# Spread row factors by a shuffle, mask the inverse in halves, rotate during the value projection, group the compression chunks by four

## Chip, cores and metric

The kernel runs on one core of one Trainium2 chip. The metric is the device time of one execution in microseconds (us), as the median of several runs. In the names of the profile, PE is the matrix engine, PEld its weight loads, DVE the vector engine, ACT the scalar engine, POOL the GpSimd engine, and SP the engine whose queue issues most DMAs.

## What is computed

One decoder block on 256 tokens of width 1024, all in float32:

```python
h = x @ w_in                      # q,k,v,z,beta,decay of DeltaNet; q, three K/V pairs, gates of NSA; merge gates
q, k = l2norm(silu(conv4(dq))), l2norm(silu(conv4(dk)));  v = silu(conv4(dv))
y_dn = gated_delta_rule(q, k, v, g, beta) ...              # chunks of 64 tokens, 8 heads
y_nsa = nsa_attention(nq, kc, vc, ksl, vsl, kwn, vwn, gates)
x = layer_norm(alpha*x + (sig(mg_dn)*(y_dn @ w_dn) + sig(mg_nsa)*(y_nsa @ w_nsa)) @ w_out)
x = layer_norm(alpha*x + (silu(u_gate) * u_val) @ w_down)  # u = conv3(x @ w_up) + b
```

Three pieces matter here. In the delta rule every chunk of 64 tokens and every head has a matrix of decays, `decay[i,j] = exp(g_i - g_j)` on a triangle, and a unit lower triangular system that is solved (`triangular_solve`). In NSA the keys and values of the compressed branch pass through `silu(blk @ w1) @ w2`, where `w1` has 4096 rows and 256 columns, once for keys and once for values. And the first 32 dims of the queries and of two sets of keys are rotated (`partial_rope`).

## The kernel before, in words

**Projections.** The order of the work is written out by hand: the list `PLAN` names 128x1024 weight chunks of 512 KB in the order in which PE uses them, and `HEAD` is its first part: `k`, `q`, `kc`, `vc`, then 16 bodies (`nq` 0 to 7, `ksl` 0 and 1, `kwn` 0 and 1, `vt` 0 to 3), each of them followed by one compression chunk `cmp`. After `HEAD` come `v`, `z`, the merge gates and the rest. Each weight chunk is loaded by SP into one of six `raw` buffers (`dma_chunk`, L167), split by ACT and DVE into a high part and a low part (`split_chunk`, L187 and L192; three buffers each), and used by 24 matmuls (`mm_feat`, L313 to L315), whose result lies in one of two PSUM buffers `pg` until ACT or DVE has read it. A new split may begin when PE is done with a chunk; a new load into `raw` when a split is done.

**Compression.** `cmp_chunk` (L775) multiplies one 128x1024 chunk of `w1`: four matmuls with 32 stationary columns each, into four groups of 32 partitions of one PSUM tile `ph`, so that the four run beside one another; each counts as two records in the profile. Eight chunks make the keys' hidden layer, eight the values'. The chunks lie in four slots in the tile `AT` (`cmp_slot`); `feed` issues their loads on SP behind the loads into `raw`.

**Fibers.** Everything else is written as generators that `pump` advances by one turn after each projection: `delta` (decays, similarities, inverse), `rope`, `cmp_end`, `attention`. `wait(name)` gives up as many turns as the tables `W` and `WAITS` say. All engines run their instructions in the order in which they were emitted; a waiting instruction holds all behind it on its engine.

**Row factors.** `delta` transposes 32 row factors per token (`rrow`, L494), writes them to DRAM (`rscr`, L498) and reads them back onto all partitions (L502, two DMAs of 512 KB into `L` and `QKT`, quarters 0 and 3 of the tile `LT`). Five turns later a mask and a column factor are added, to `L` by DVE and to `QKT` by POOL (L509, L511), ACT takes both exponentials, and the similarities are multiplied in (L521 to L528) for four groups of heads and tokens, one PSUM buffer each of the four named `ps`.

**Inverse.** POOL inverts the 16x16 diagonal blocks (L570, L572), writes the result and its transpose to DRAM (`tscr`, L577), reads them back in another layout (L580), and four turns later DVE, POOL and ACT spread them under a mask over `T` and `TT` (L588, L590).

**Rotation.** `rope` starts after `HEAD`. It loads 768 KB of cosines and sines, gathers 32 rows of `NQ` and `KC` with eight DMAs into `AT`, runs four DVE instructions of 768 columns (L734 to L739) and scatters the result with eight DMAs (L741, L743).

Of the kernel before, what the change touches and what calls it, by code (L numbers as in the profile page):

```python
# [6 lines left out]
F32 = mybir.dt.float32  # L7
# [26 lines left out]
def _slots(table, *items):  # L34
    o = 0
    for name, n in items:
# [8 lines left out]
              ("fcb", 44), ("g1", 8), ("b1", 8), ("w2", 512))  # L45
N_PA = 169
TAIL = 7
# [15 lines left out]
def plan():  # L63
# [4 lines left out]
    for j in range(NFF):  # L68
        seq += [("ug", j), ("uv", j)]
        if 0 < j <= NFF - TAIL:  # L70
# [10 lines left out]
         wc=0, sv=0, wv=0, lc=0, s3=1, s4=1, ss=0, z=0, on=0, oc=1, sim=1, vb=1, rest=0, zz=1)  # L81
WAITS = dict(back0=4, ca0=2, ca1=0, cb0=2, cb1=5, expL0=0, expQ0=0, la0=2, la2=1, la3=3, later0=0, later1=1,
             later3=2, lb0=1, lb1=2, lb2=2, lb3=0, lc0=0, lc1=0, lev0=3, mask0=5, oc0=2, oc1=1, oc2=0, oc3=0,
             on0=0, p400=2, pgm0=3, rb0=4, rest0=2, rows0=1, s10=0, s30=1, s32=1, s34=0, s36=8, s37=0, s41=2,
             s42=3, s43=2, sa2=2, sc0=1, sc2=1, sc3=1, sim0=2, sim2=0, sim3=0, ss0=2, step2=0, sv0=0, t400=1,
# [8 lines left out]
CMP_LEAD = 6  # L94


class Body:
# [72 lines left out]
    def cmp_slot(self, n):  # L170
        return self.AT[:, 1024 * (n % 4):1024 * (n % 4) + 1024]

# [58 lines left out]
    def feed(self):  # L231
        held = lambda: [*self.raw, *(i for i, h in self.plain.items() if h)]
        while self.n_dma < len(GEMM) and self.n_dma - min(held(), default=self.n_dma) < 6:
            self.dma_chunk(self.n_dma)
            self.n_dma += 1
        if self.n_split >= CMP_LEAD and self.n_cmp < 16:
            while self.n_cmp < min(16, self.cmp_done + 4):
                self.nc.sync.dma_start(self.cmp_slot(self.n_cmp), self.A["w"][CMP[self.n_cmp]])
                self.n_cmp += 1

# [217 lines left out]
    def delta(self):  # L458
# [35 lines left out]
        nc.vector.tensor_copy(rrow, pr[0:32, 0:128])  # L494
        scr = self.dram.tile([2, 2, 16, 64], F32, name="rscr")
        lq = self.LT.rearrange("p (w n) -> p w n", w=4)[:, 0:4:3]
        for w in range(2):
            nc.gpsimd.dma_start(scr[w].rearrange("e u t -> u e t"),  # L498
                                rrow[16 * w:16 * w + 16].rearrange("u (e t) -> u e t", e=2))
        yield from self.wait("rw")  # L500
        for e in range(2):
            nc.gpsimd.dma_start(lq[64 * e:64 * e + 64], bass.AP(tensor=scr.tensor, offset=scr.offset + 1024 * e,  # L502
                                                                ap=[[0, 64], [2048, 2], [1, 1024]]))
        yield from self.wait("mask")
        bc = lambda t, n, m: t[:, :, None].to_broadcast([128, n, m])
        for eng, dst, m, b in ((nc.vector, L, "mL", bL), (nc.gpsimd, QKT, "mQ", Rk)):
            for hf in range(2):
                us = slice(8 * hf, 8 * hf + 8)
                eng.tensor_tensor(dst[:, us], dst[:, us], self.cp(m)[:, None, :].to_broadcast([128, 8, 64]),  # L509
                                  op=OP.add)  # L510
                eng.tensor_tensor(dst[:, us], dst[:, us], bc(b[:, us], 8, 64), op=OP.add)  # L511
        yield from self.wait("expL")
        self.act(L, L, AF.Exp)
        yield from self.wait("expQ")
        self.act(QKT, QKT, AF.Exp)
        for c in range(4):
# [50 lines left out]
        for j in range(15):  # L567
# [9 lines left out]
        nc.gpsimd.dma_start(st.rearrange("w u (b i) j -> (u b) w (i j)", b=8),  # L577
                            vf[:, 512:1024].rearrange("p (w i) -> p w i", w=2))
        yield from self.wait("tw")
        nc.gpsimd.dma_start(vf[:, 0:512].rearrange("p (n j) -> p n j", j=16),  # L580
                            st.rearrange("w u p j -> p (w u) j"))
        yield from self.wait("back")
        tp = self.LT[:, 1024:3072].rearrange("p (n j) -> p n j", j=64)
        tc = vf[:, 0:512].rearrange("p (n j) -> p n j", j=16)
        for b, eng in enumerate((nc.vector, nc.gpsimd, nc.vector, None)):
            o = tp[:, :, 16 * b:16 * b + 16]
            if eng:
                eng.tensor_scalar(o, tc, bm[:, b:b + 1], None, op0=OP.mult)  # L588
            else:
                self.act(o, tc, AF.Copy, scale=bm[:, b:b + 1])  # L590
        yield from self.wait("lev")
# [127 lines left out]
    def rope(self):  # L719
        nc = self.nc  # L720
        while "nsa_in" not in self.flags:
            yield
        AT = self.AT
        cs = AT[:, 0:1536]
        r = AT[:, 1536:2304]
        rs = AT[:, 2304:3072]
        nc.sync.dma_start(cs, self.A["rope"])
        for j in range(4):
            nc.sync.dma_start(r[32 * j:32 * j + 32, 0:512].rearrange("p (a t) -> p a t", a=2),
                              self.NQ[0:32, 2 * j:2 * j + 2])  # L730
            nc.sync.dma_start(r[32 * j:32 * j + 32, 512:768], self.KC[0:32, j // 2, j % 2])
        yield from self.wait("ra")
        co = cs[:, :768]
        nc.vector.tensor_tensor(co, r, co, op=OP.mult)  # L734
        nc.vector.stream_shuffle(rs, r, [(i + 16) % 32 for i in range(32)])
        yield from self.wait("rd")
        nc.vector.tensor_tensor(rs, rs, cs[:, 768:], op=OP.mult)
        yield from self.wait("rc")
        nc.vector.tensor_tensor(r, co, rs, op=OP.add)  # L739
# [27 lines left out]
    def cmp_chunk(self, i):  # L767
        nc = self.nc
        w, part = divmod(i, 8)
        wv = self.cmp_slot(i).rearrange("p (l c) -> p l c", l=4)  # L770
        if part == 0:
            self.ph = self.psum.tile([128, 512], F32, name="ph", tag="o", bufs=1)[:, :256]
        src = self.pe_view(w, part // 4).rearrange("p g (n l) -> p (g n) l", l=16)
        for l in range(4):
            nc.tensor.matmul(self.ph[32 * l:32 * l + 32], src[:, :, (4 * part + l) % 16], wv[:, l],  # L775
                             start=(part == 0), stop=(part == 7), skip_group_check=True)
        self.cmp_done += 1
        self.feed()
# [209 lines left out]
    def run(self):  # L988
# [22 lines left out]
        def evac_v(pg, h):  # L1011
            self.conv(pg, self.Z[:, h], cw[:, 16 + h])

        evs = dict(k=evac_qk(0), q=evac_qk(1), kc=self.evac_cmp(0), vc=self.evac_cmp(1), v=evac_v,
                   nq=cps(lambda j: self.NQ[:, j]), ksl=cps(lambda j: self.KC[:, j, 0]),
                   kwn=cps(lambda j: self.KC[:, j, 1]))
        for kind, j in HEAD:
# [6 lines left out]
            elif (kind, j) != ("k", 1):  # L1024
                self.feat(kind, j, X, evs[kind])
            if (kind, j) == ("k", W["smalls"]):
                self.start(sm)
            if (kind, j) == ("q", 7):
                self.drain("ws")
                self.flags.add("q")  # L1030
                V = self.V = self.mem.tile([128, 8, 256], F32, name="V", tag="v", bufs=1)
                self.start(self.delta(), True)
        self.flags.add("nsa_in")
        self.start(self.rope())
        self.start(self.attention(), True)
# [306 lines left out]
def _layout(i):  # L1342
# [85 lines left out]
    ct, st = angles(np.arange(S))  # L1428
    out["rope"] = np.concatenate([np.tile(ct, (4, 3)), np.tile(st, (4, 3))], 1)
    out["cpk"] = cp  # L1430
# [34 lines left out]
```

## Time and profile before

| | |
|---|---|
| time, median of 3 runs (lowest to highest) | 576.69 us (576.42 to 577.76) |
| the profiled execution's own time | 577.12 us |
| its span, from the first instruction to the last | 575.3 us |
| busy: PE / PEld / DVE / ACT / POOL | 561.3 / 507.5 / 391.6 / 301.5 / 106.5 us |
| DMA traffic | 101.87 MB, mean 177 GB/s |

A row of the timeline has the start in us from the span's start, the time, the engine, the line of the kernel, the operation, the tiles written and read, the shapes, the count, and in brackets how long the engine had been idle and what ended the wait. Matmuls overlap, so the distance of two starts tells what one costs PE, not its duration. A group of the view by lines has busy time and the mean duration of one in ns. The DMA view has the count, the size, and the median time from issue to landing.

### The profile page before, as it was taken

The page shows a single profiled execution, that of the slowest core. Times are in us where ns is not written, and L with a number is a line of the kernel's source. Part 1 is how long each engine was busy: PE and PEld are TensorE (multiplying, and loading weights), DVE is VectorE, ACT ScalarE, POOL GpSimd, SP SyncE. Part 2 cuts the span into 40 slices and gives each one's busy share as a digit, 9 for nine tenths or more (in the row PEclk, how much of TensorE's full clock was granted, in tenths as well). Part 3 has the DMA queues.
Part 4 walks back from the last instruction along what each step waited for, and adds up shares of the span by engine and source line. Part 5 has one row for each costly group of instructions (what it writes and reads, how often), then busy time and mean ns, then how long its engine had stood idle before and what let it go on. Part 6 is the DMA issues. An engine that isn't in the chain of part 4 may idle for free.

```text
span 575.3 us, 11562 instructions
## 1 busy us (share of the span) xinstructions
PE 561.3 (98%) x4589; PEld 507.5 (88%) x4589; DVE 391.6 (68%) x674; ACT 301.5 (52%) x550; POOL 106.5 (19%) x133
## 2 busy tenths in 40 slices
PE   9999999999989999999999999999999999999994
PEld 6999988877989998888988799899999999999974
DVE  2888743684986653467657477778777777778884
ACT  4655643334454556554676344375555555556651
POOL 2466601405510220003000000059000000000003
PEclk9999999999999999999999999999999999999998
DMA  8965577965763233223353635825655555555601
GB/s 306 407 250 169 165 236 248 321 220 165 253 173 107 94 111 111 75 74 111 111 185 131 236 127 174 282 78 181 219 185 185 187 184 190 189 185 179 201 7 73
DMA packets 28790, 101.87 MB, mean 177 GB/s; under 512 B 3424, under 2 KB 4224, under 8 KB 28352
## 3 DMA queue, kind: packets, MB, share of 16 engines
q1 hardware_dynamic: 27696, 96.85, 50.0%
q0 software_dynamic: 896, 3.95, 2.4%
q8 instruction: 36, 0.59, 0.4%
q10 hardware_dynamic: 144, 0.33, 0.1%
q14 instruction: 18, 0.15, 0.1%
HBM read 98.87 MB, written 1.46 MB: 174 GB/s over the span
## 4 chain that ended last, share of the span: by engine, by line
PE 82%; DVE 9%; ACT 4%; DMA 3%; issue 1%; SPq 0%; DVEq 0%; ACTq 0%
PE pg L313 18%; PE pg L314 17%; PE pg L315 17%; PE pdn L1228 3%; PE pdn L1229 3%; PE pdn L1227 3%; DMA raw<-in_w 2%; DVE lo L192 2%; PE poa L921 2%; PE ph L775 1%; PE psa L861 1%; PE pwo L963 1%; PE pwo L964 1%; PE pwo L962 1%; ACT hi L187 1%
## 5 line engine op out<-in xcount | busy, mean ns | idle before, releaser
L192 DVE TENSOR_TENSOR lo<-raw,hi 128x1024 fp32r<-128x1024 f32 (+1 forms) x147 | 178.9, 1219 | 85.9 <-ACT hi L187 82.6
L187 ACT CAST hi<-raw 128x1024 fp32r<-128x1024 f32 (+1 forms) x151 | 154.6, 1029 | 41.1 <-PE pg L314 13.4
L313 PE MATMUL pg<-X,hi 128*128 128x256 f32 x496 | 144.2, 291 | 1.7 <-DVE Z L345 1.7
L314 PE MATMUL pg<-X,hi 128*128 128x256 f32 x496 | 139.5, 281 | 0.0
L315 PE MATMUL pg<-X,lo 128*128 128x256 f32 x496 | 139.5, 281 | 0.0
L313 PE MATMUL pg<-Y,hi 128*128 128x256 f32 x400 | 113.0, 283 | 0.0
L314 PE MATMUL pg<-Y,hi 128*128 128x256 f32 x400 | 112.7, 282 | 0.0
L315 PE MATMUL pg<-Y,lo 128*128 128x256 f32 x400 | 112.5, 281 | 0.0
L313 PEld LDWEIGHTS pg<-X,hi 128*128 128x128 f32 x496 | 93.3, 188 | 10.6 <-issue 7.3
L314 PEld LDWEIGHTS pg<-X,hi 128*128 128x128 f32 x496 | 93.5, 188 | 0.3 <-issue 0.2
L315 PEld LDWEIGHTS pg<-X,lo 128*128 128x128 f32 x496 | 93.4, 188 | 0.0
L314 PEld LDWEIGHTS pg<-Y,hi 128*128 128x128 f32 x400 | 75.3, 188 | 0.3 <-issue 0.2
L313 PEld LDWEIGHTS pg<-Y,hi 128*128 128x128 f32 x400 | 75.3, 188 | 0.2 <-issue 0.2
L315 PEld LDWEIGHTS pg<-Y,lo 128*128 128x128 f32 x400 | 75.3, 188 | 0.0
L1303 POOL TENSOR_TENSOR NQ<-NQ,AT 128x512 f32<-128x512 f32 x2 | 2.6, 1294 | 159.7 <-ACT NQ L143 159.7
L1228 PE MATMUL pdn<-lo,X 128*128 128x512 f32 (+1 forms) x90 | 31.6, 351 | 0.0
L1227 PE MATMUL pdn<-hi,X 128*128 128x512 f32 (+1 forms) x90 | 31.5, 350 | 0.0
L1229 PE MATMUL pdn<-hi,X 128*128 128x512 f32 (+1 forms) x90 | 31.4, 349 | 0.0
L345 DVE SCALAR_TENSOR_TENSOR uv<-pg,ppk,uv 128x255 f32<-128x255 f32 (+1 forms) x44 | 21.2, 481 | 11.0 <-ACT uv L143 9.8
L345 DVE SCALAR_TENSOR_TENSOR cv<-pg,ppk,cv 128x255 f32<-128x255 f32 (+2 forms) x48 | 23.1, 481 | 8.0 <-ACT cv L143 6.9
L882 POOL TENSOR_SCALAR AT<-AT,sums 128x128 f32<-128x128 f32 (+1 forms) x12 | 10.9, 920 | 88.1 <-DVE sums L874 51.0
L1267 ACT CAST X<-ug 128x256 fp32r<-128x256 f32 x22 | 8.9, 407 | 33.2 <-DVE ug L1263 33.2
(338 smaller groups left out, 932.2 us busy)
## 6 DMA issues: line engine op xcount, KB each, us to landing
raw<-in_w SPq DMA_DIRECT2D x156, 512.0 KB, 4.0
AT<-in_w SPq DMA_DIRECT2D x16, 512.0 KB, 6.6
AT<-in_first SPq DMA_DIRECT2D x3, 512.0 KB, 6.7
LT<-rscr POOLq DMA_DIRECT2D x2, 512.0 KB, 9.9
V<-in_xk POOLq DMA_DIRECT2D x1, 1024.0 KB, 5.5
KD<-in_lnp POOLq DMA_DIRECT2D x1, 1024.0 KB, 6.2
AT<-in_lnp SPq DMA_DIRECT2D x1, 1024.0 KB, 8.4
AT<-in_rope SPq DMA_DIRECT2D x1, 768.0 KB, 5.9
```

Source lines behind the costliest of these rows:

```text
L187: nc.scalar.copy(hi[:, o:o + n], raw[:, o:o + n])
L192: nc.vector.tensor_tensor(lo[:, :n], raw[:, :n], hi[:, :n].bitcast(F32), op=OP.subtract)
L313: nc.tensor.matmul(pg, hi[:, k], src[:, 0, k], start=(k == 0), stop=False)
L314: nc.tensor.matmul(pg, hi[:, k], src[:, 1, k], start=False, stop=False)
L315: nc.tensor.matmul(pg, lo[:, k], src[:, 0, k], start=False, stop=(k == 7))
L345: nc.vector.scalar_tensor_tensor(dst[:, s:], pg[:, :S - s], cw[:, n - 1 - s:n - s], dst[:, s:], op0=OP.mult, op1=OP.add)
L882: (nc.vector, nc.gpsimd)[b].tensor_scalar(e, e, w, None, op0=OP.mult)
L921: nc.tensor.matmul(po, self.VT[:, b % 2, c0:c0 + 128], PT[:, b].rearrange("p i q -> p (i q)"), start=False, stop=(b == bs[-1]))
L1227: nc.tensor.matmul(p, fh[:, ts], hi[:, sl], start=(j == 0), stop=False)
L1228: nc.tensor.matmul(p, fh[:, ts], lo[:, sl], start=False, stop=False)
L1229: nc.tensor.matmul(p, fl[:, ts], hi[:, sl], start=False, stop=(j == NFF - 1))
L1267: nc.scalar.copy(fh, f)
```

## The change

The order of `HEAD` becomes four bodies, then four compression chunks, four times over. The slots for compression chunks become six (two of them in `Z`, whose first use comes later), and `feed` issues at most one such load per call, ahead of the loads into `raw`; `cmp_chunk` no longer calls `feed`.

The row factors go to two partitions of each half only (four DMA rows of 8 KB in two DMAs, into a zeroed part of `LT`), and a DVE shuffle spreads each over its 32 partitions. Mask and column factor are added up on POOL beforehand (into `KD`), so that DVE adds one tile to `L` and one to `QKT`; this comes three turns after the row factors instead of five, and the second exponential one turn after the first. The inverse is written and read in two halves (`TT` first), masked one turn later, by DVE and ACT alone.

The rotation's input is a second ACT copy of 32 partitions out of PSUM, made beside each copy of `nq`, `ksl` and `kwn`, into three quarters of a tile of `V`; the cosines and sines are loaded once (256 KB) after the first `nq`. The fiber starts after `kwn` 1, so its DVE work comes beside `vt`; it sets its flag at the same turn as before.

```diff
-    for i, b in enumerate(body):
-        seq += [b, ("cmp", i)]
+    for i in range(0, 16, CMP_GROUP):
+        seq += body[i:i + CMP_GROUP] + [("cmp", i + j) for j in range(CMP_GROUP)]
...
-WAITS = dict(back0=4, ... expQ0=0, ... mask0=5, ... rb0=4, ...)
+WAITS = dict(back0=5, ... expQ0=1, ... mask0=3, ... rb0=11, ra0=1, ...)
...
     def feed(self):
+        if self.n_split >= CMP_LEAD and self.n_cmp < min(16, self.cmp_done + CMP_SLOTS):
+            self.nc.sync.dma_start(self.cmp_slot(self.n_cmp), self.A["w"][CMP[self.n_cmp]])
+            self.n_cmp += 1
         while self.n_dma < len(GEMM) and ... < 6:
...
-        if self.n_split >= CMP_LEAD and self.n_cmp < 16:
-            while self.n_cmp < min(16, self.cmp_done + 4):
...
+        nc.gpsimd.memset(self.LT[:, 1024:3072], 0.0)
...
-        for w in range(2):
-            nc.gpsimd.dma_start(scr[w]..., rrow[16 * w:16 * w + 16]...)
+        nc.gpsimd.dma_start(scr.rearrange("e u t -> u e t"), rrow.rearrange("u (e t) -> u e t", e=2))
...
         for e in range(2):
-            nc.gpsimd.dma_start(lq[64 * e:64 * e + 64], bass.AP(..., ap=[[0, 64], [2048, 2], [1, 1024]]))
+            nc.gpsimd.dma_start(seed[64 * e:64 * e + 33:32], bass.AP(..., ap=[[0, 2], [1, 2048]]))
...
-                eng.tensor_tensor(dst[:, us], dst[:, us], mask, op=OP.add)
-                eng.tensor_tensor(dst[:, us], dst[:, us], bc(b[:, us], 8, 64), op=OP.add)
...
+                nc.gpsimd.tensor_tensor(kd[:, w, us], mask, bc(b[:, us], 8, 64), op=OP.add)
+        yield from self.wait("mask")
+        for w, dst in enumerate((L, QKT)):
+            nc.vector.stream_shuffle(flat, seed[:, 1024 * w:1024 * w + 1024], [0] * 32)
+            nc.vector.tensor_tensor(dst, dst, kd[:, w], op=OP.add)
+            yield from self.wait("expQ" if w else "expL")
+            self.act(dst, dst, AF.Exp)
...
-        for b, eng in enumerate((nc.vector, nc.gpsimd, nc.vector, None)):
...
+        for w, dst in ((1, TT), (0, T)):
+            for b in range(4):
+                if b % 2:
+                    self.act(o, tc, AF.Copy, scale=bm[:, b:b + 1])
+                else:
+                    nc.vector.tensor_scalar(o, tc, bm[:, b:b + 1], None, op0=OP.mult)
...
-        nc.sync.dma_start(cs, self.A["rope"])
-        for j in range(4):
-            nc.sync.dma_start(r[...], self.NQ[0:32, 2 * j:2 * j + 2])
-            nc.sync.dma_start(r[...], self.KC[0:32, j // 2, j % 2])
+        r, rs, cs = self.r, self.V[:, 5:8]..., self.V[:, 0:2]
...
+        def evac_rot(dst, slot):
+            def evac(pg, j):
+                nc.scalar.copy(dst(j), pg)
+                q, a = slot(j)
+                nc.scalar.copy(self.r[32 * q:32 * q + 32, 256 * a:256 * a + 256], pg[0:32])
...
+            if (kind, j) == ("kwn", 1):
+                self.flags.add("nsa_in")
+                self.start(self.rope())
...
-        self.flags.add("nsa_in")
-        self.start(self.rope())
```

## Rows read from the trace of the kernel before

**Rows 1.** The page: the span, and PE's busy time, share and instructions.
```profile
span 575.3 us, 11562 instructions
PE 561.3 (98%) x4589; PEld 507.5 (88%) x4589; DVE 391.6 (68%) x674; ACT 301.5 (52%) x550; POOL 106.5 (19%) x133
```

**Rows 2.** Timeline of PE around one compression chunk.
```profile
77.80 0.28 PE L315 MATMUL pg<-X,lo 128*128 128x256 f32 x1
78.01 0.67 PE L775 MATMUL ph<-AT,misc 128*32 128x256 f32 x8
78.61 0.38 PE L313 MATMUL pg<-X,hi 128*128 128x256 f32 x1
78.83 0.28 PE L314 MATMUL pg<-X,hi 128*128 128x256 f32 x1
78.95 0.27 PE L315 MATMUL pg<-X,lo 128*128 128x256 f32 x1
```

**Rows 3.** Groups by line and shape, PE: all compression matmuls.
```profile
L775 PE MATMUL ph<-AT,misc 128*32 128x256 f32 x128 | 10.7, 407 | 0.0
```

**Rows 4.** Timeline of PE: two runs of half-width matmuls behind one another.
```profile
218.36 1.09 PE L650 MATMUL px<-ST,QK 128*64 128x128 f32 x16
219.29 1.04 PE L650 MATMUL po<-ST,QK 128*64 128x128 f32 x16
```

**Rows 5.** Timeline of all engines, 104.5 to 116.6 us: masks, exponentials, first similarities.
```profile
106.76 1.79 DVE L509 TENSOR_TENSOR LT<-LT,cpk 128x512 f32<-128x512 f32 x1
...
113.18 2.00 ACT L143 ACTIVATE LT<-LT 128x1024 f32<-128x1024 f32 x2 [7.60 <-DVE LT L511]
114.09 0.66 PE L525 MATMUL pk<-cpk,QK 128*128 128x128 f32 x4
...
115.21 0.69 DVE L527 TENSOR_TENSOR LT<-psim,LT 128x512 f32<-128x512 f32 x1 [2.07 <-ACT LT L143]
...
115.96 0.63 PE L792 MATMUL phs<-cpk,hp 128*128 128x30 f32 x4 [1.22 <-DVE LT L527]
```

**Rows 6.** Timeline of all engines, 120 to 124 us: the last similarities.
```profile
120.16 1.09 PE L521 MATMUL psim<-QK 128*64 128x128 f32 x16
...
121.18 0.66 PE L525 MATMUL pk<-cpk,QK 128*128 128x128 f32 x4
...
121.77 1.09 PE L521 MATMUL psim<-QK 128*64 128x128 f32 x16
122.76 0.69 DVE L527 TENSOR_TENSOR LT<-psim,LT 128x512 f32<-128x512 f32 x1
```

**Rows 7.** Timeline of all engines, 156.5 to 162.3 us: rotation and masks beside `v`.
```profile
156.73 0.95 DVE L734 TENSOR_TENSOR AT<-AT 128x768 f32<-128x768 f32 x1
...
157.60 1.06 DVE L735 STREAM_SHUFFLE AT<-AT 128x768 f32<-128x768 f32 x1
...
160.21 0.28 PE L315 MATMUL pg<-X,lo 128*128 128x256 f32 x1
...
160.57 1.51 DVE L345 SCALAR_TENSOR_TENSOR Z<-pg,ppk,Z 128x255 f32<-128x255 f32 x3
...
162.17 0.72 ACT L143 ACTIVATE LT<-VN,cpk 128x512 f32<-128x512 f32 x1 [4.26 <-DMA VN<-tscr]
...
162.22 0.36 PE L313 MATMUL pg<-X,hi 128*128 128x256 f32 x1 [1.74 <-DVE Z L345]
```

**Rows 8.** Timeline of POOL ahead of the row factors.
```profile
89.33 1.28 POOL L498 DMA_DIRECT2D rscr<-rrow  x2 [16.12 <-DVE rrow L494]
```

**Rows 9.** DMA issues from 92 to 108 us.
```profile
AT<-in_w SPq DMA_DIRECT2D x5, 512.0 KB, 9.5
LT<-rscr POOLq DMA_DIRECT2D x2, 512.0 KB, 9.9
```

**Rows 10.** DMA issues from 76 to 90 us.
```profile
AT<-in_w SPq DMA_DIRECT2D x4, 512.0 KB, 4.7
```

**Rows 11.** Line L238, all loads of compression chunks.
```profile
DMA to landing us min/median/max: 4.1/6.6/11.4
```

More of the change, by code (lines that the diff above doesn't have):

```diff
@@ L46 @@
 N_PA = 169
+CMP_GROUP = 4
+CMP_SLOTS = 6
 TAIL = 7
@@ L170, in cmp_slot @@
     def cmp_slot(self, n):
-        return self.AT[:, 1024 * (n % 4):1024 * (n % 4) + 1024]
+        n %= CMP_SLOTS
+        home, n = (self.AT, n) if n < 4 else (self.Z.rearrange("p h t -> p (h t)"), n - 4)
+        return home[:, 1024 * n:1024 * n + 1024]
     def split_chunk(self, i):
@@ L500, in delta @@
         yield from self.wait("rw")
         for e in range(2):
-            nc.gpsimd.dma_start(lq[64 * e:64 * e + 64], bass.AP(tensor=scr.tensor, offset=scr.offset + 1024 * e,
-                                                                ap=[[0, 64], [2048, 2], [1, 1024]]))
-        yield from self.wait("mask")
+            nc.gpsimd.dma_start(seed[64 * e:64 * e + 33:32], bass.AP(tensor=scr.tensor, offset=scr.offset + 2048 * e,
+                                                                     ap=[[0, 2], [1, 2048]]))
@@ L505, in delta @@
         bc = lambda t, n, m: t[:, :, None].to_broadcast([128, n, m])
-        for eng, dst, m, b in ((nc.vector, L, "mL", bL), (nc.gpsimd, QKT, "mQ", Rk)):
+        kd = self.KD.rearrange("p u j -> p (u j)").rearrange("p (w u j) -> p w u j", w=2, u=16)
+        for w, (m, b) in enumerate((("mL", bL), ("mQ", Rk))):
             for hf in range(2):
                 us = slice(8 * hf, 8 * hf + 8)
-                eng.tensor_tensor(dst[:, us], dst[:, us], self.cp(m)[:, None, :].to_broadcast([128, 8, 64]),
-                                  op=OP.add)
-                eng.tensor_tensor(dst[:, us], dst[:, us], bc(b[:, us], 8, 64), op=OP.add)
@@ L512, in delta @@
[L512 to L515, printed above, removed]
+                nc.gpsimd.tensor_tensor(kd[:, w, us], self.cp(m)[:, None, :].to_broadcast([128, 8, 64]),
+                                        bc(b[:, us], 8, 64), op=OP.add)
+        yield from self.wait("mask")
+        for w, dst in enumerate((L, QKT)):
+            flat = dst.rearrange("p u j -> p (u j)")
+            nc.vector.stream_shuffle(flat, seed[:, 1024 * w:1024 * w + 1024], [0] * 32)
+            nc.vector.tensor_tensor(dst, dst, kd[:, w], op=OP.add)
+            yield from self.wait("expQ" if w else "expL")
+            self.act(dst, dst, AF.Exp)
@@ L722, in rope @@
             yield
[L723 to L726, printed above, removed]
-        nc.sync.dma_start(cs, self.A["rope"])
-        for j in range(4):
-            nc.sync.dma_start(r[32 * j:32 * j + 32, 0:512].rearrange("p (a t) -> p a t", a=2),
-                              self.NQ[0:32, 2 * j:2 * j + 2])
-            nc.sync.dma_start(r[32 * j:32 * j + 32, 512:768], self.KC[0:32, j // 2, j % 2])
+        r, rs, cs = self.r, self.V[:, 5:8].rearrange("p h t -> p (h t)"), self.V[:, 0:2]
         yield from self.wait("ra")
-        co = cs[:, :768]
-        nc.vector.tensor_tensor(co, r, co, op=OP.mult)
+        v3 = lambda t: t.rearrange("p (a t) -> p a t", a=3)
+        angle = lambda w: cs[:, w:w + 1].to_broadcast([128, 3, 256])
         nc.vector.stream_shuffle(rs, r, [(i + 16) % 32 for i in range(32)])
         yield from self.wait("rd")
-        nc.vector.tensor_tensor(rs, rs, cs[:, 768:], op=OP.mult)
+        nc.vector.tensor_tensor(v3(r), v3(r), angle(0), op=OP.mult)
+        nc.vector.tensor_tensor(v3(rs), v3(rs), angle(1), op=OP.mult)
         yield from self.wait("rc")
-        nc.vector.tensor_tensor(r, co, rs, op=OP.add)
+        nc.vector.tensor_tensor(r, r, rs, op=OP.add)
         for j in range(4):
@@ L777, in cmp_chunk @@
         self.cmp_done += 1
-        self.feed()
         if part == 7:
@@ L1012, in evac_v @@
             self.conv(pg, self.Z[:, h], cw[:, 16 + h])
+        def evac_rot(dst, slot):
[3 more added lines that the diff above has]
+                nc.scalar.copy(self.r[32 * q:32 * q + 32, 256 * a:256 * a + 256], pg[0:32])
+            return evac
         evs = dict(k=evac_qk(0), q=evac_qk(1), kc=self.evac_cmp(0), vc=self.evac_cmp(1), v=evac_v,
-                   nq=cps(lambda j: self.NQ[:, j]), ksl=cps(lambda j: self.KC[:, j, 0]),
-                   kwn=cps(lambda j: self.KC[:, j, 1]))
+                   nq=evac_rot(lambda j: self.NQ[:, j], lambda j: (j // 2, j % 2)),
+                   ksl=evac_rot(lambda j: self.KC[:, j, 0], lambda j: (2 * j, 2)),
+                   kwn=evac_rot(lambda j: self.KC[:, j, 1], lambda j: (2 * j + 1, 2)))
         for kind, j in HEAD:
@@ L1025, in run @@
                 self.feat(kind, j, X, evs[kind])
+            if (kind, j) == ("nq", 0):
+                nc.sync.dma_start(V[:, 0:2].rearrange("p h t -> p (h t)"), A["rope"])
+            if (kind, j) == ("kwn", 1):
+                self.flags.add("nsa_in")
+                self.start(self.rope())
             if (kind, j) == ("k", W["smalls"]):
@@ L1428, in _layout @@
     ct, st = angles(np.arange(S))
-    out["rope"] = np.concatenate([np.tile(ct, (4, 3)), np.tile(st, (4, 3))], 1)
+    out["rope"] = np.concatenate([np.tile(ct, (4, 1)), np.tile(st, (4, 1))], 1)
     out["cpk"] = cp
```

33 lines of the change are left out of this document (13 added, 20 removed).

## The prediction

> **What bounds the kernel now.** I read the page first: PE is busy for 561.3 of 575.3 us [rows 1], and in the order of its own instructions. So the time is the sum of what PE is given, plus its waits, and any other engine matters only where PE waits for it. A busy share hides two things that the timeline of PE shows by the distance of starts: waits, and what it costs to go from one kind of matmul to another. I looked for both in the part that the change touches, from the first `nq` (about 70 us) to the first `z` (about 166 us).
>
> The kinds of matmul first. Projection matmuls start 0.12 us apart (78.83, 78.95). Around a compression chunk the distance from the last full-size step before it to the second one after it is 78.83 - 77.80 = 1.03 us [rows 2]. Two ordinary steps are 0.24, so a lone chunk costs PE 0.79 us. Its work is less: eight records are two passes of four matmuls side by side, 256 columns each. The rest is the way into the narrow form (0.21 instead of 0.12) and out of it (the second step after it 0.22 instead of 0.12, and a slow first and last pass).
>
> What does a pass cost inside a longer stretch? Sixteen half-width records are eight passes of 128 columns; a run of them starts 0.93 us before the next run of the same form (218.36 to 219.29) [rows 4], that is 0.116 per pass, start-up included, so at most 0.23 for 256 columns. I take 0.22. The other end comes from the lone chunk itself: it lasts 0.67 us with a mean record of 0.407, so its second pass starts at most 0.27 behind the first [rows 2, 3].
>
> Then the waits. Two are inside the touched part. At 114.09 `pk` starts and the next PE work comes 1.87 us later, released by DVE's multiplication at L527 [rows 5]; the same step elsewhere takes 0.59 (121.18 to 121.77) [rows 6]. That is 1.28 us lost: DVE waited for ACT's exponentials, and ACT had been idle 7.60 us for the mask additions, which began at 106.76. At 160.21 a `v` projection ends and the next begins at 162.22 [rows 7], 1.89 us more than the ordinary step: its PSUM buffer was held until DVE had done the convolution, which began at 160.57 because rotation had occupied DVE since 156.73.
>
> **The change part by part, and the sum.** The profiled execution took 577.12 us, 1.8 more than its span and 0.4 above the median of 576.69; I subtract from the median.
>
> *Four stretches.* Twelve of the sixteen chunks lose their way in and out. Each such chunk falls from 0.79 to two inner passes, 0.44, which is 0.35 saved, 12 x 0.35 = 4.2 us. By the slow bound (0.27 per pass) it is 12 x 0.25 = 3.0; if the array emptied again between chunks it would be nothing. Against it stand five short jobs of PE (`pgm`, the square sums, the second similarity, `phs`, `pc`) that stood directly before a chunk and shared its way out. They now return to a projection by themselves, about 0.1 each (the 0.22 against 0.12 above): 0.5 us back.
>
> *Row factors.* The two 512 KB reads go, and seeds of 32 KB come. DVE's shuffle of 768 columns took 1.06 us [rows 7], so 1024 columns are some 1.4, and an addition of 768 columns 0.95, so 1024 are about 1.25. For `L` and `QKT` together DVE needs 5.3 us, where its four additions, from 106.76 to the release of ACT at 113.18, took 6.4 beside POOL. The work comes two turns earlier. I reckon the times as follows: the projection `nq` 6 ends near 94.6 us in the new order, DVE is done with its split by 98, `L` is ready at 101, `QKT` at 103.5. ACT is held at the first exponential until 101, and behind it stands the evacuation of `nq` 7, whose buffer PE wants back for `ksl` 1 near 104, as a stretch of compression lies between. So the 1.28 us go. The seeds lie outside the trace: they land at best like the fast loads (4.1) and at worst like the old reads (9.9) [rows 9, 11]; issued near 92, the value I take is under 5, as they are small, and then they are there before 98. POOL's zeroing of 2048 columns has no row; it may cost several us and still be hidden, since POOL stood idle 16.12 us before the row factors [rows 8].
>
> What is late next: `phs`. In the new order the last two similarities and `phs` fall into one turn, and `phs` needs the buffer of the first of them. At 120.16 the same pair began and DVE's L527 on the first was done at 122.76 + 0.69 = 123.45, 3.3 us later [rows 6]. A second ACT copy now stands ahead of the split (0.3), so 3.6; PE arrives after 2 x (1.02 + 0.59) = 3.2. I add 0.4 us.
>
> *Rotation.* DVE's four instructions (156.73 to 160.57) move to `vt`, where DVE has no convolutions, and the `v` stretch loses them and its wait: 1.89 us. Twelve extra ACT copies, up to 0.4 each, lie beside projections, with ACT busy for only 52% of the span [rows 1]; if that cover were gone they would cost up to 4.8. The eight scatters and their wait stand ahead of four loads on SP; those loads have six buffers, some 17 us, and lose about 6.
>
> *Inverse.* In `v`, ACT stood 4.26 us for the data of the inverse [rows 7]. One more turn, an earlier start and halves take that wait away. PE did not wait for it beyond the 1.89, so I count nothing more. ACT gets four masks of half the size where it had one of 0.72; about 1 us, against a free buffer.
>
> Sum: -4.2 + 0.5 - 1.3 + 0.4 - 1.9 = -6.5 us, which gives 570.2 us. From `z` on the work of PE is the same and only earlier.
>
> **The rivals.**
>
> *B. The stretch doesn't run faster than lone chunks.* Then only the waits go: -1.3 - 1.9 + 0.4 = -2.8, 573.9 us. For it: no row shows more than two passes of the 32-column form behind one another. Against it: the half-width form does run on evenly [rows 4].
> The Trainium skill speaks for this rival (TensorE: Matmul & The Clock Gate, The mechanism): a weight load overlaps matmuls in flight only where it goes to another group of rows, and all these loads use all rows. By that rule each pass would wait for its weights, the gain of the stretches would go, and the sum would be that of B. The trace does not agree in the full-size form, where a 0.28 us record starts every 0.12.
>
> *C. Compression loads come late; slower than before.* Six slots hold four chunks of this stretch and two of the next, so two of the next are loaded while four projections run, and the last of them only in the second call of `feed`: behind a load that waits for a split, about 6.2 us after the stretch. It is needed about 13 us after it, so a landing above 6.8 us stops PE, in three of the stretches. With the longest landing seen, 11.4 [rows 11], it costs 3 x 4.6 = 13.8, and the time is 584 us; the change is lost from a landing of 9 on. For it: between 92 and 108 us such loads took 9.5 [rows 9]. Against it: the two reads of 512 KB were under way then, which the change takes out; shortly before, they took 4.7 [rows 10]. Two chunks may now stand behind one another in the queue, which I put at one more us, still under 6.8.
>
> *D. Seeds late.* If they land after 9.9 us, the shuffle starts 3.6 us later, and `ksl` 1 waits about 2.1 for its buffer; 572.3 us, or 574 if the shuffle is also dearer than its row.
>
> **Chances.** The forecast (all terms as summed) 0.66, its own range 568.5 to 572.0, from inner passes between 0.21 and 0.27 and the new wait between 0 and 0.8. B 0.14, D 0.12, C 0.08. A difference of 0.3%, 1.7 us, is what a measurement of this kernel can tell from none. The forecast and most of B and D lie beyond it: faster 0.84. A part of B and D with another small wait, and a mild C, make no difference: 0.08. The rest of C, and what I overlook, is slower: 0.08. For 8 times in 10 the range reaches over D and B: 568.3 to 574.3.
>
> **What would show it.** In the new timeline of PE four rows of L775 with 32 records each, about 1.9 us from the first of them to the next projection; if one takes 2.4 or more, B holds. No PE wait before `phs` longer than 0.5 us and none on `Z` between `v` projections. ACT's wait before the first exponential under 5 us. Loads of compression chunks landing in 4 to 6 us throughout; a PE wait for one of them at the head or in the middle of a stretch would be C, and a wait of `ksl` 1 for ACT would be D. The prediction is wrong if the stretch from `nq` 1 to the first `z` is not 6 to 7 us shorter, or if it is and the time beyond `z` grows.

## Result, and the profile after

The changed kernel takes **571.5 us** (median of 4 runs, 571.29 to 572.34) against 576.92 for the kernel before on the same chip (576.42 to 577.76): 0.9906 of its time, 95% interval 0.9884 to 0.9928. It is 5.4 us faster, where 6.5 were forecast, and lies 1.3 above the predicted 570.2. The profiled execution took 571.39 us.

The page of the kernel after; these rows answer to [rows 1]:

```profile
span 569.6 us, 11567 instructions
PE 557.0 (98%) x4589; PEld 508.1 (89%) x4589; DVE 392.9 (69%) x678; ACT 307.2 (54%) x565; POOL 106.6 (19%) x134
```

PE has as many matmuls as before and is busy 4.3 us less. Where the span became shorter is seen from the starts of the same projection in both traces (first matmul of it, us from the span's start):

| projection | before | after | difference | forecast up to here |
|---|---|---|---|---|
| `nq` 0 | 70.5 | 70.5 | 0 | 0 |
| `v` 0 | 138.67 | 135.43 | -3.24 | -4.6 |
| `v` 7 | 162.22 | 157.26 | -4.96 | -6.5 |
| `z` 0 | 166.33 | 161.31 | -5.02 | -6.5 |
| end of the span | 575.3 | 569.6 | -5.7 | -6.5 |

So the stretch with the compression gave 1.4 us less than forecast, the `v` stretch gave 1.7 to 1.8 where 1.9 was said, and 0.7 came where nothing was said: 0.65 of it between `z` 0 and 186 us, in steps of 0.1 to 0.4, each too short for the list of waits. In `v` the wait gave its 1.90 in full (162.22 against 157.26, beside the projection before); 0.17 was lost ahead of it, because from 144.5 us on the projection matmuls of this execution start 0.120 apart where those of before start 0.1185. Why is open; the profiled executions of e9 and e12 don't show it.

The stretch itself, in the timeline of PE after (compare [rows 2]):

```profile
83.52 0.29 PE L318 MATMUL pg<-X,lo 128*128 128x256 f32 x1
84.19 0.28 PE L496 MATMUL pr<-cpk,rcat 128*32 128x128 f32 x1 [0.38 <-DVE rcat L483]
84.40 1.97 PE L773 MATMUL ph<-AT,misc 128*32 128x256 f32 x32
86.29 0.39 PE L316 MATMUL pg<-X,hi 128*128 128x256 f32 x1
86.52 0.28 PE L317 MATMUL pg<-X,hi 128*128 128x256 f32 x1
```

The reader is to see 32 records, four chunks, that start 1.89 us before the next projection. A lone chunk before took 0.60 (78.01 to 78.61). Six more passes thus cost 1.29, 0.215 each. The row above the stretch is new: the row transpose `pr` waits for DVE, and no chunk stands ahead of it any more to cover that.

The list of PE's waits in the kernel after (line, cause, total in us, count, longest), without those of the kernel's start and of its later parts:

```profile
PE pg L316 <- ACT V L1015: 0.6, 1, 0.6
PE phs L789 <- DVE LT L531: 0.5, 1, 0.5
...
PE pr L496 <- DVE rcat L483: 0.4, 1, 0.4
```

The wait on `Z` in `v` and the wait behind `pk` are gone; three small ones took their place. The first of them in the timeline of all engines after, 94 to 106 us (compare [rows 5] and [rows 8]):

```profile
94.14 1.23 DVE L196 TENSOR_TENSOR lo<-raw,hi 128x1024 fp32r<-128x1024 f32 x1 [1.63 <-ACT hi L191]
94.37 1.13 POOL L504 DMA_DIRECT2D LT<-rscr  x2 [4.82 <-DMA rscr<-rrow]
...
95.53 2.07 POOL L511 TENSOR_TENSOR KD<-cpk,bL 128x512 f32<-128x512 f32 x2
...
96.99 3.71 DVE L196 TENSOR_TENSOR lo<-raw,hi 128x1024 fp32r<-128x1024 f32 x1 [1.62 <-ACT hi L191]
97.56 2.06 POOL L511 TENSOR_TENSOR KD<-cpk,rcat 128x512 f32<-128x512 f32 x2
...
100.63 1.31 DVE L516 STREAM_SHUFFLE LT<-LT 128x1024 f32<-128x1024 f32 x1
...
102.04 1.23 DVE L517 TENSOR_TENSOR LT<-LT,KD 128x1024 f32<-128x1024 f32 x1
...
103.30 1.06 ACT L145 ACTIVATE LT<-LT 128x1024 f32<-128x1024 f32 x1 [6.34 <-DVE LT L517]
...
104.63 0.36 ACT L1015 COPY V<-pg 32x256 f32<-32x256 f32 x1
```

DVE's split, 1.23 us at 94.14, takes 3.71 at 96.99 while POOL adds masks. The shuffle starts behind it at 100.63, so `L` is ready at 103.3 and not at 101, and the evacuation of `nq` 7 stands behind the exponential until 104.99, which is what `ksl` 1 waits for. The seeds had been written from 88.77 (landed +5.04) and read from 94.37 (landed +4.85): they were there at 99.2 and 99.4.

And the `v` stretch after, all engines (compare [rows 7]):

```profile
156.34 1.73 ACT L145 ACTIVATE LT<-VN,cpk 128x256 f32<-128x256 f32 x4 [1.53 <-DMA VN<-tscr]
...
156.48 1.30 DVE L595 TENSOR_SCALAR LT<-VN,cpk 128x256 f32<-128x256 f32 x4
...
157.26 0.28 PE L316 MATMUL pg<-X,hi 128*128 128x256 f32 x1
...
158.47 1.52 DVE L348 SCALAR_TENSOR_TENSOR Z<-pg,ppk,Z 128x255 f32<-128x255 f32 x3 [0.37 <-ACT Z L145]
```

Rotation is gone from here, ACT waits 1.53 for the inverse instead of 4.26, and `v` 7 starts without a wait at 157.26.

### The profile page after: what moved, and what is told of

It reads as the page before. It is cut to its first block, busy times and chain, and to the rows that moved or that the text cites. A ratio compares the mean times of both kernels' runs of the same rounds, so it can differ in the third digit from the quotient of the medians.

```text
span 569.6 us, 11567 instructions
## 1 busy us (share of the span) xinstructions
PE 557.0 (98%) x4589; PEld 508.1 (89%) x4589; DVE 392.9 (69%) x678; ACT 307.2 (54%) x565; POOL 106.6 (19%) x134
## 4 chain that ended last, share of the span: by engine, by line
PE 89%; DVE 5%; ACT 3%; DMA 2%; issue 1%; SPq 0%; DVEq 0%; ACTq 0%
PE pg L316 19%; PE pg L317 19%; PE pg L318 19%; PE pdn L1237 3%; PE pdn L1238 3%; PE pdn L1236 3%; PE poa L918 2%; PE psa L858 2%; PE pwo L961 1%; PE pwo L960 1%; PE pwo L959 1%; DVE lo L196 1%; ACT hi L191 1%; DMA AT<-in_first 1%; PE ph L773 1%
## 5 line engine op out<-in xcount | busy, mean ns | idle before, releaser
L196 DVE TENSOR_TENSOR lo<-raw,hi 128x1024 fp32r<-128x1024 f32 (+1 forms) x147 | 181.4, 1236 | 78.2 <-ACT hi L191 76.8
```

The source lines that it names most:

```text
L196: nc.vector.tensor_tensor(lo[:, :n], raw[:, :n], hi[:, :n].bitcast(F32), op=OP.subtract)
```

## Experiments

Each kernel is the changed kernel with one edit, unless said otherwise, and was timed in five rounds beside the kernel before. PE's wait for its very first loads varied from 0.2 to 2.0 us between executions, as much as some of the effects. So I also give how far two profiles are apart at the end once the difference at `nq` 0 (70 us) is taken off; I call that *aligned*.

**1. Chunks alone, and in pairs.**

```diff
-CMP_GROUP = 4
+CMP_GROUP = 1     # e1;  = 2 in e2
```

> The changed kernel with each compression chunk again behind its own projection; all else of the change stays. Theory (twelve ways into and out of the narrow matmul form are what the grouping saves, 0.34 us each, less 0.4 for short jobs that used to share one): the time rises by 3.0 to 3.9 us against the changed kernel, to 574.5 to 575.4 us, and the 16 chunks stand as 16 rows of 8 records, 0.60 us each. Rival (the gain came from the two waits, and the grouping is neutral, since the changed kernel has new waits of 0.45 and 0.7 us): it stays within 1 us of 571.5.

> The changed kernel with the compression chunks in eight pairs. Theory (a price per way in and out): four ways more than with stretches of four, so 1.0 to 1.6 us more, 572.5 to 573.1 us; a pair lasts about 1.03 us from its start to the next projection (0.60 + 2 x 0.216). Rival (the gain needs a long stretch, since the first passes of any stretch are slow): the pair costs as much as two lone chunks, and the time is that of the kernel with lone chunks.

In pairs: 572.87 us, ratio to before 0.9926 (0.9911 to 0.9941), aligned +1.55. Four more stretches at 0.35 are 1.4: as expected. A two-chunk stretch takes 1.03 us in its trace (76.98 to 78.01), and 0.60, 1.03 and 1.89 for one, two and four chunks lie on one line with 0.215 per pass. Alone: 577.65, ratio 0.9996 (0.9981 to 1.0012), some 2.5 more than expected; its runs lie in two groups, near 575.5 and near 578, and the profile, aligned +4.8, is from the lower one. Timeline of ACT and PE in that kernel:

```profile
103.64 1.06 ACT L145 ACTIVATE LT<-LT 128x1024 f32<-128x1024 f32 x1 [5.50 <-DVE LT L517]
...
106.31 1.05 ACT L145 ACTIVATE LT<-LT 128x1024 f32<-128x1024 f32 x1
...
107.26 0.35 ACT L778 COPY hp<-ph 128x256 f32<-128x256 f32 x1
...
107.67 0.67 PE L773 MATMUL ph<-AT,misc 128*32 128x256 f32 x8 [2.48 <-ACT hp L778]
```

The eighth chunk ends the keys' hidden layer, whose copy stands behind the second exponential, and the ninth needs its buffer. Without that wait 2.3 are left; and the waits of `pr` and `ksl` 1 (1.0 together) are absent from this kernel's list. So the grouping itself is worth some 3.3 aligned, where 3.7 was summed (4.2 - 0.5). Rival B is false. Of the upper group no trace was kept; the mean granted clock of six of its seven executions is 0.989 to 0.995, that of the five lower ones 0.997 or 0.998, so the clock may have fallen in the upper ones; that is not shown.

**2. The grouping without the rest** (kernel before, with only the new order, the slots and `feed`).

```diff
+    for i in range(0, 16, CMP_GROUP):
+        seq += body[i:i + CMP_GROUP] + [("cmp", i + j) for j in range(CMP_GROUP)]
...
+CMP_SLOTS = 6     # and the new feed(); WAITS, row factors, rotation, inverse as before
```

> The kernel before with nothing but the four stretches (order of the head, six slots, one load per call ahead of the others). Theory: 4.1 saved, 0.4 back, and a wait of about 0.45 at the transpose of the row factors, which now has no chunk in front of it; the two old waits (1.3 before phs, 1.9 in v) stay in some size: 3.0 to 3.8 us below before, 573.1 to 573.9 us. Rival (neutral grouping): within 1 us of before.

581.98 us, ratio 1.0087 (1.0064 to 1.011): slower than before by 5, though it should have been 3 to 4 faster. Its DMA view, 92 to 108 us, a row of its timeline of PE, and one of its table by stretches (time, busy and count of PE, PEld, DVE, ACT, POOL, then PE's granted clock, DMA share and GB/s):

```profile
raw<-in_w SPq DMA_DIRECT2D x4, 512.0 KB, 9.7
LT<-rscr POOLq DMA_DIRECT2D x2, 512.0 KB, 12.4
...
```

```profile
118.28 1.06 PE L794 MATMUL phs<-cpk,hp 128*128 128x30 f32 x4 [7.03 <-DVE LT L530]
```

```profile
118.28:124.03 5.75, 5.75 (x27) 5.75 (x28) 4.96 (x8) 1.77 (x4) 0.00 (x0) 0.50 0.52 178
```

The two reads of row factors, issued at 94.64 and 95.23, landed at 104.70 and 109.88; masks began at 109.97, and exponentials ended at 117.5, when PE had run out of other work. Two things add up here. PE loses 7.1 us there (110.60 to 118.28, less the ordinary 0.59), where the kernel before lost 1.28: 5.8 more. And from 113.8 to 124.0 us, that is from within this stop, the granted clock is 0.50, the lower level (1.2 GHz): `phs` takes 0.88 to the next start instead of 0.37, and the 24 projection matmuls behind it start 0.21 apart instead of 0.12, some 2.7 us more. At `v` 0 the kernel is 4.6 behind the kernel before (aligned), so an estimated 3.9 were gained elsewhere: the grouping gives its gain here too, and the late row factors, with the clock behind them, take 8.5. The rest of the difference at the end comes before `z` 0, where PE waits 1.2 for a mask of the inverse. So the edit by itself costs 5 us, and pays only with the seeds of 8 KB rows, which land by 99.4 in the changed kernel. The parts of the change are not a sum that can be taken one by one.

**3. Rotation earlier again.**

```diff
-WAITS = dict(... rb0=11, ra0=1, ...)
+WAITS = dict(... rb0=4, ra0=8, ...)
```

> The changed kernel with the rotation's DVE work and scatters given seven turns later, so that they fall behind the fifth v projection as they did before; all else of the change stays. Theory (DVE's 3.9 us there held the PSUM buffer): the wait between v projections returns with about 1.9 us, 573.0 to 573.6 us. Rival (the wait came from ACT, which stood for the data of the inverse, and that is shorter now): at most 0.5 us more.

573.74, ratio 0.9937 (0.9923 to 0.9951), just above the 573.6 expected, aligned +2.3. Timeline, all engines:

```profile
153.45 1.05 DVE L732 STREAM_SHUFFLE V<-V 128x768 f32<-128x768 f32 x1
...
156.39 0.96 DVE L737 TENSOR_TENSOR V<-V 128x768 f32<-128x768 f32 x1
...
157.27 1.51 DVE L348 SCALAR_TENSOR_TENSOR Z<-pg,ppk,Z 128x255 f32<-128x255 f32 x3
...
158.92 0.36 PE L316 MATMUL pg<-X,hi 128*128 128x256 f32 x1 [1.72 <-DVE Z L348]
```

The four rotation instructions fill DVE before a convolution, and PE waits 1.72 for it: the wait of [rows 7], brought back by this one move. The term of 1.9 is shown.

**4. The inverse one turn earlier, as before.**

```diff
-WAITS = dict(back0=5, ...)
+WAITS = dict(back0=4, ...)
```

> The changed kernel with the inverse's masks given one turn earlier, as before the change, but still in halves. Theory (the data of the inverse land near 156 us, and ACT, standing for them, holds the next convolution): ACT waits about 4 us, PE waits 2 to 3 us between v projections, 573.5 to 574.5 us. Rival (halves alone are enough, the extra turn is idle): under 0.5 us more than the changed kernel.

577.49, ratio 0.9985 (0.9965 to 1.0006): the whole gain is gone, more than either theory said. The list of PE's waits:

```profile
PE pg L316 <- DVE Z L348: 2.6, 1, 2.6
PE pg L316 <- ACT V L1015: 1.4, 1, 1.4
```

A row of its table by stretches, in the order of the one above:

```profile
162.02:165.43 3.41, 3.41 (x22) 3.19 (x22) 2.52 (x5) 0.20 (x1) 0.00 (x0) 0.50 0.43 154
```

ACT then waits 4.23 for the halves (156.96), with the evacuation of a `v` projection behind it, the convolution starts only at 159.09, and PE, done with `v` 6 at 158.1, waits 2.61 for its buffer. The second wait (ACT, 1.4) is that of `ksl` 1, larger than the 0.6 of the kernel after, though nothing was changed there: the seeds landed at 101.3 in this execution and not at 99.4. Aligned, the kernel is 0.9 behind at `ksl` 1, 3.5 at `v` 7, 5.0 at `z` 0 and 6.0 at the end. Between `v` 7 and `z` 0 no wait is in the list; there the granted clock is 0.50 from 162.0 to 165.4 us, behind the wait of 2.61, and the projection matmuls start 0.21 apart instead of 0.12, which makes 1.4. Why the last 1.0 is lost stays open. So the extra turn, which I had counted at nothing, carries 2.6 us of wait and, in this execution, 1.4 of clock behind it, once rotation is gone.

**5. POOL's additions, the row transpose, and both.** In e5 and e7 the four POOL additions stand before the row transpose; in e6 and e7 the square sums come one turn earlier and the transpose keeps its turn.

```diff
# e5, e7: nc.gpsimd.tensor_tensor(kd[...]) x4 moved ahead of
         yield from self.wait("rows")
# e6, e7:
-WAITS = dict(... rows0=1, ... ss0=2, ...)
+WAITS = dict(... rows0=2, ... ss0=1, ...)
```

> The changed kernel with POOL's four additions of mask and column factor put before the transpose of the row factors, so that they run near 85 to 89 us instead of 95.5 to 99.6. Theory (DVE's split of 3.71 us in the changed kernel was held by those additions, and the seeds land only just before it ends): that split takes 1.2 us again, but another one, near 87 us, is held instead, and the copy of the row factors behind it comes 1 to 2 us later, so the seeds land near 100 to 101 us and the time moves by less than 0.5 us either way. Rival (POOL's additions held nothing, the split was slow by itself): a split near 97 us still takes over 3 us.

> The changed kernel with the sums of squares gathered one turn earlier and the transpose of the row factors left at its turn. Theory (the transpose waits 0.45 us since no compression chunk stands in front of it any more): that wait goes, 0.3 to 0.5 us less, 571.0 to 571.2 us; the wait of 0.6 us for the evacuation behind the first exponential stays. Rival (PE would only wait for something else): no change.

> Both of the edits: sums of squares one turn earlier and POOL's additions ahead of the transpose, where they now run near 81 to 85 us beside no split that matters. Theory: no split over 1.8 us before the shuffle, the shuffle starts when the seeds land, about 1.2 us earlier than in the changed kernel, and both small waits of PE (0.45 and 0.6 us) go: 570.2 to 570.7 us. Rival (the seeds' landing sets the shuffle, and it has not moved): only the 0.45 goes, 571.1 us.

573.46 (ratio to before 0.9924, 0.9897 to 0.995), 572.18 (0.9902, 0.9875 to 0.993) and 572.85 (0.9916, 0.9887 to 0.9945); aligned +1.4, -0.68 and +0.98. The `pr` wait goes in e6, as it should; the medians cannot show 0.7. In e5 and e7 the split behind `nq` 6 takes 1.23 again, so POOL's additions are what stretched it, but the time gets worse: DVE now waits 3.9 and 4.1 us for the seeds, which land at 101 to 103, and `ksl` 1 waits 2.1 and 2.3.

**6. The additions on other data.** To take the contention away without moving the seeds, the additions were made on a constant, long before; the masks of this kernel leave the column factors out.

```diff
+        nc.gpsimd.memset(fake, -2000.0)
+        ...  tensor_tensor(kd[:, w, us], mask, bc(fake[:, us], 8, 64))    # x4, ahead of wait("ss")
-                nc.gpsimd.tensor_tensor(kd[:, w, us], mask, bc(b[:, us], 8, 64), op=OP.add)
```

> The four additions of POOL (mask + row value) are done on a constant instead of the row values, and ahead of everything else in the row factors, when POOL is idle; so the masks of L and QKT are not the reference's. They no longer stand beside DVE's split at 97 us, nor behind the row transpose or ahead of the seeds' issue. Theory (contention between POOL's additions and DVE's split, 3.71 us instead of 1.23, is what makes the shuffle late): the split takes 1.23 again, the shuffle starts when the seeds land, 99.0 to 99.5 on the scale of the changed kernel, instead of 100.6; the wait of ksl 1 falls from 0.6 to 0 and the time by 0.4 to 0.7 us, 570.8 to 571.1. Rival (the DMA hops of the seeds hold the shuffle anyway, about 5 us each, and what POOL does only moves them): the seeds land at 101 or later as in the two kernels with the additions moved, ksl 1 waits 1.5 us or more, and the time is 572 to 573.

571.86, ratio 0.9919 (0.9894 to 0.9943), aligned +0.3; the same as the changed kernel. Timeline of DVE:

```profile
96.92 1.23 DVE L196 TENSOR_TENSOR lo<-raw,hi 128x1024 fp32r<-128x1024 f32 x1 [1.62 <-ACT hi L191]
100.61 0.01 DVE L518 LOAD_MASK_SELECT LT<-LT  x1 [2.47 <-DMA LT<-rscr]
100.64 1.31 DVE L518 STREAM_SHUFFLE LT<-LT 128x1024 f32<-128x1024 f32 x1
```

The split is short, and the shuffle starts at 100.64, as with the long one (100.63): the seeds landed at 99.05 and 100.49. My theory falls; the two hops through DRAM hold the shuffle as well. In the kernel after, split and seeds end within 1.3 us of each other, so an end of the contention alone can be worth at most those 1.3, and here it was worth nothing: the seeds were read 0.5 later and landed 1.1 later than in the kernel after.

**7. Small waits moved.** e9 puts the masks one turn later, so that the evacuation of `nq` 7 stands ahead of them on ACT; e10 adds the edit of e6 and puts `phs` one turn later.

```diff
-WAITS = dict(... ca0=2, ... expQ0=1, ... mask0=3, ...)
+WAITS = dict(... ca0=2, ... expQ0=0, ... mask0=4, ...)                         # e9
+WAITS = dict(... ca0=3, ... expQ0=0, ... mask0=4, ... rows0=2, ... ss0=1, ...) # e10
```

> One turn is put between the masks and where they stand now (mask0 3 to 4) and taken out again behind them (expQ0 1 to 0): the evacuation of nq 7 then stands ahead of the first exponential on ScalarE, and the similarities keep their turn. Theory (the 0.6 us that ksl 1 waits is paid because the shuffle is late and the evacuation stands behind the exponential): that wait goes, nothing else changes, 570.7 to 571.2 us, 0.5 below the changed kernel. Rival (the exponentials are themselves what comes next): the first similarity product or phs waits instead, 0.5 us or more longer than now, and the time stays at 571.5 or rises above it.

> Three small waits moved at once: the row transpose one turn later (ss0 2 to 1, rows0 1 to 2), the masks one turn later as in the kernel before this one, and phs one turn later (ca0 2 to 3). If the waits 0.4 (before the row transpose), 0.6 (ksl 1) and 0.5 (phs) are each a price of the order and independent, all three go and the time is 569.9 to 570.5 us. If they are one chain (the DVE work of this stretch is simply late by half a microsecond), one of them comes back at the next step and the time is 571 or more. What phs gains can also be lost where its readers are now late: then a new wait stands before pc or a query similarity.

e9: 570.59, ratio 0.9891 (0.9872 to 0.9911), the lowest median of all; the wait of `ksl` 1 is off its list, `ksl` 1 starts 0.72 earlier aligned, and 0.4 is left at the end. That it is faster than the changed kernel is not shown: the two ratios' intervals overlap (0.9884 to 0.9928 there). e10: 574.22, ratio 0.9956 (0.9938 to 0.9973): of its three waits two are gone and that of `ksl` 1 is 0.4, and aligned it is 1.7 us ahead of the changed kernel at `v` 7. Then, in the list of PE's waits and in the timeline:

```profile
PE pg L316 <- DVE Z L348: 1.9, 1, 1.9
```

```profile
157.52 0.91 ACT L145 ACTIVATE LT<-VN,cpk 128x256 f32<-128x256 f32 x2 [4.75 <-DMA VN<-tscr]
...
159.96 1.51 DVE L348 SCALAR_TENSOR_TENSOR Z<-pg,ppk,Z 128x255 f32<-128x255 f32 x3 [0.36 <-ACT Z L145]
```

The inverse on POOL begins with a write and a read through DRAM. In e10 the write was issued earlier than in the changed kernel, at 119.45 instead of 120.49, but took 6.1 us instead of 4.2, and the read, issued at 126.07 instead of 125.27, took 5.1 instead of 3.1: two loads of 512 KB now follow the write within 1.8 us, where there were 2.6 us without any, and one stands 0.4 us ahead of the read. The data were there 2.8 us later, and ACT waits 4.75 for the inverse, as in e8. Behind PE's wait of 1.9, from 161.2 to 164.6 us, the granted clock is 0.50, and 14 projection matmuls start 0.21 apart instead of 0.12: 1.25 us more. The wait and the clock are most of the 3.7 lost between `v` 7 and the end. The hidden path, POOL's inverse with its four hops, ends close behind PE, and I take it that an earlier PE brings its loads into these hops; that is read from one execution of each kernel. Which of the three edits did it was not separated.

**8. Four slots for chunks.**

```diff
-CMP_SLOTS = 6
+CMP_SLOTS = 4
```

> CMP_SLOTS 6 to 4: no chunk of the next stretch can be loaded until one of the present stretch is done, so the loads come 2 chunks later. If loads were what the stretches hang on (rival C: the changed kernel escapes only because two chunks are loaded early), PE waits for a chunk's load at the head of the later stretches, 1 to 5 us in each of up to three: 574 to 585 us, and the records show PE waits on AT<-in_w. If the queue has room to spare, as landings of 4.6 to 8.5 us let me think, against some 13 us between two stretches, no such wait appears and the time is 571.3 to 571.9 us.

573.69, ratio 0.9951 (0.9928 to 0.9973); the profiled execution was the longest of seven, 576.41 (the shortest 573.03). Its list of PE's waits, and a table of the stretch around the second one (time, busy and count of PE, PEld, DVE, ACT, POOL, then PE's granted clock, DMA share and GB/s):

```profile
PE ph L773 <- DMA AT<-in_w: 3.0, 2, 1.9
```

```profile
136.50:138.50 2.00, 0.05 (x5) 0.00 (x1) 1.72 (x2) 0.15 (x1) 1.84 (x3) 1.00 0.40 124
138.50:139.27 0.77, 0.77 (x9) 0.23 (x9) 0.00 (x0) 0.00 (x0) 0.61 (x3) 0.74 0.09 19
139.27:142.20 2.93, 2.93 (x17) 2.93 (x14) 0.00 (x0) 0.37 (x1) 2.38 (x8) 0.50 0.34 85
142.20:144.50 2.30, 2.30 (x21) 2.30 (x21) 0.24 (x1) 0.74 (x2) 1.75 (x8) 0.98 0.70 223
```

This is rival C, made real by two slots fewer: the last chunk of two stretches lands at 103.02 and 138.45, and PE waits 1.08 and 1.95 for it. It cost 4.1 us aligned in this execution, more than the two waits: behind the second the granted clock was 0.50, the lower level (1.2 GHz), up to 142.3 us, and 13 projection matmuls started 0.21 apart instead of 0.12, 1.3 us more. With six slots the loads land after 4.4 to 10.2 us (median 6.8) and PE waits for none: the slow ones are issued long before their stretch, and the last load of each of the last three stretches takes 4.6, 6.4 and 4.4 us and lands 3.3, 4.3 and 2.9 before its use.

## Why the prediction was right or wrong

*What bounds the kernel: right.* PE's order and its waits explain the difference but for 0.65 us beyond `z` 0, 0.17 in `v` and 0.25 ahead of `v` 0.

*Four stretches: right in size.* 0.215 per inner pass (0.22 was taken) and 0.35 per joined chunk, by e2 and by the three lengths of a stretch. A pass of 256 columns takes 0.215 and one of 128 columns 0.116 [rows 4], so nearly all of it goes with the columns and some 0.02 is left for anything else, while a weight load of a chunk lasts 0.143 in the mean. The Trainium skill's rule (TensorE: Matmul & The Clock Gate, The mechanism), that a weight load overlaps only with matmuls of another group of rows, does not hold for these passes, whose loads all use all rows; the same section also names a background weight buffer as a case in which a load is pulled ahead, and the measured passes fit that.

*What the chunks had covered: mis-sized.* 0.5 us were given back for five short jobs that had shared a chunk's way out. I did not look at what the chunk ahead of such a job does for its *operands*: the row transpose lost the 0.79 us in which DVE finished `rcat`, and waits 0.4. e6 shows it, since the wait goes when the operand is ready a turn earlier.

*Row factors: the step that failed.* The 1.28 us did go. But "DVE is done with its split by 98, `L` is ready at 101" was wrong by 2.3, for two causes that hit the same moment. The first is the seeds: I had one hop of under 5 us from an issue near 92, but there are two in a row, the write from 88.77 and the read from 94.37, and they are there at 99.4. The second is POOL: its additions made the split last to 100.70. The trace of before had this in view: one DVE addition took 1.79 beside POOL [rows 5], where a same-sized multiplication, one of whose inputs lies in PSUM, took 0.69, and I used that row for the old place alone. The Trainium skill has such a rule (GPSIMD Engine Reference, Specifications): POOL's SBUF interface is shared with VectorE, and DVE instructions with two SBUF inputs contend; the split is one, and 3.71 against 1.23 agrees. Taking the second cause away leaves the wait as it is (0.6 in e12, with seeds 1.1 later), or makes it longer where the seeds come later still (e5, e7); seeds that come earlier by themselves were not tried. So what I wrote for D, `ksl` 1 waiting for its buffer behind the exponential, came about within the forecast, with seeds that landed in 4.5 to 4.9 and not 9.9.

*`phs`: right*, 0.5 for 0.4. *Rotation: right*, by e4. *Inverse: right as a sum, wrong as a reason.* It was costed at nothing, and e8 shows 2.6 us of wait and 1.4 of lower clock behind that zero. ACT's wait for the inverse did no harm of its own only as long as rotation's wait stood there; without the extra turn the gain in `v` would have been lost. *Beyond `z`* 0.65 more came than the nothing forecast; its place is known, its cause was not tried. The largest step, 0.35 at 185.4 us, is at `psa`, behind a DVE multiplication (L621 in the kernel after) that starts with `psc` in the kernel after and 0.48 behind it in the kernel before; in e2 and e12 `psa` waits 0.2 for it.

The sum, then: -6.5 forecast, +0.4 for `pr`, +0.6 for `ksl` 1, +0.1 for `phs`, +0.2 in `v`, -0.75 beyond `v` 7, gives -5.95 against -5.7 in the two spans. The 0.25 left over lies ahead of `v` 0 and is not located.

*The signs, and luck.* By its own main sign the prediction misses: the stretch up to the first `z` was to become 6 to 7 us shorter, and from `nq` 0 it is 5.0 (`nq` 1 itself starts a chunk earlier in the new order). ACT's wait before the first exponential is 6.34 where under 5 was said, and loads of chunks took up to 10.2 where 4 to 6 was said. The time lies inside the forecast's own range all the same, by luck: without the 0.65 beyond `z`, which nothing in the sum foresaw, it would be 572.15 (an estimate), above the 572.0 where that range ends.

## What to carry to other kernels

When short jobs are gathered into one long stretch, list for every job that stood beside them what the gap had covered: its operands as well as its way into and out of an array form. Before an edit is taken over by itself, ask which other edit makes room for it; here the edit was 5 us slower alone, its gain of 3 to 4 taken by a wait that had been short before, and the grouping is worth some 3 beside the small row factors. And work that is said to be hidden behind a wait has no price only for as long as that wait stays; price it again for the case that the wait is removed. Last, when a slower kernel has no wait in the list that explains the loss, look at the granted clock behind its waits: in e3, e8, e10 and e11 it was part of the price.

## What the runs showed of the hardware that was not expected

- A DVE split of 128x1024 (two inputs in SBUF) took 3.71 us beside POOL additions of 128x512, and 1.23 without them.
- A read of the seeds, 16 KB in rows of 8 KB, took 4.2 to 6.0 us from issue to landing in all kernels but e1 (3.1), about what the 512 KB loads into `raw` took in the same stretch (3.6 to 5.0 in the changed kernel); two 512 KB reads issued into a busier stretch took 10.1 and 14.7 (e3).
- Behind some PE waits the granted clock fell to 0.50 and cost more, each in the one profiled execution: 1.3 us behind 1.95 (e11), 1.25 behind 1.9 (e10), 1.4 behind 2.61 (e8), some 2.7 around 7.03 (e3). Behind others as long it stayed at 1.00: 1.74 before [rows 7], 1.72 in e4, 2.1 in e5, 2.3 in e7, 2.48 in e1. The length of the wait alone does not tell the two apart.
